# Two-layer hybrid encoder on one core: five small moves, and a copied first weight tile for each up run of the MLP

## The chip, the cores and the metric

The kernel runs on one core of one Trainium2 chip. A core has TensorE for matrix products (PE; its weight loads are shown as PEld), VectorE (DVE), ScalarE (ACT), GpSimd (POOL) and SyncE (SP), which run their own instruction streams and wait for each other on semaphores. Operands lie in SBUF, 128 partitions wide; sums of products lie in PSUM, in banks of 512 float32 per partition. The metric is the device time of one execution in microseconds, as the median of several runs.

## The reference

The computation is a two-layer encoder on 256 tokens of width 2048, with 256 memory tokens beside them. All is float32.

```python
def reference(x, mem, ...):
    m = rms_norm(mem, mem_norm)
    h = x
    for i in range(DEPTH):                      # 2 layers
        n = rms_norm(h, attn_norm[i])
        if i % 2 == 0:                          # layer 0: neighbourhood attention, 12 heads
            z = n @ a_w_in[j]                   # 2048 x 5120: q, k, v and the memory heads' q
            mix = neighbourhood_attention(q, k, v, a_rpb[j])
        else:                                   # layer 1: grouped-query attention, 12 heads, 4 kv heads
            z = n @ b_w_in[j]                   # 2048 x 3072
            mix = gqa_block_attention(rope(q), rope(k), v)
        km, vm = jnp.split(m @ w_mem_kv[i], 2, axis=-1)
        cross = memory_attention(qm, km, vm)    # 4 heads into the memory tokens
        h = h + jnp.concatenate([mix, cross], axis=-1) @ w_o[i]
        n = rms_norm(h, mlp_norm[i])
        h = h + jnp.square(jax.nn.relu(n @ w_up[i])) @ w_down[i]    # 2048 -> 8192 -> 2048
    return rms_norm(h, final_norm)
```

## The kernel before

**Products in three parts.** Every float32 operand is split into a high part (ACT, a Copy to the rounded type, line 377) and a low part (DVE, source minus high part, line 378): the function `split`. A product is then three matmuls: high by high, high by low, low by high. The function `products` (line 293) makes the S works, whose weights in PE are a 128x128 piece of the weight matrix and whose moving operand is 256 tokens wide: 16 steps k of three matmuls, 48 in a whole run. `m_products` (lines 272, 275, 276) makes the M works, where the activations are in PE and 512 columns of the weight matrix move.

**Stages.** The memory's K and V for both layers come first (to about 100 us), from `memT`, then layer 0's projections and attention, its output projection, its MLP (from about 438 us), then the same for layer 1, with its output projection at about 1300 us and its MLP at about 1364 us, and the final norm.

**The attention** of one head is three steps, `attend` (scores and softmax, lines 428 to 430), `attend2` (four transposes, line 454, then a split into `pT`) and `attend3` (the products `av` with the values, lines 462 to 464, and the split into `cat`). The steps are put between the works of the plan.

**The output projection** (`add_o`) is 16 M works: four blocks of 512 columns, two at a time, each with four chunks of the contraction. Each work has two halves (`hf` 0 and 1), a half holds two steps k. In the kernel before, the eighth work from the end, in layer 1, carries the mark `behind`: both of its splits are issued only after the last head's `pT` split. A finished block is added to `h` by DVE (line 725).

**The MLP** is cut into 8 parts of 1024 hidden columns. An up run is one S work of 128 hidden columns: `uh` and `ul` are the high and low parts of its weights, `hT` the normalised activations, `ps_u` the sum. Part 0 has eight up runs one after another. From part 1 on each up run stands between two groups of down products `p` (lines 894, 896, 897; 512 wide): 7 parts of 8 runs in each layer, 112 runs in all. The down products use a Strassen scheme, whose operands are `b` and its splits `bh`, `bl`, and the sums `t` and their splits `th`, `tl`; one of the sums is made by an accumulating DMA on POOL's queue (`b<-b`, line 866). In part 0 the splits of some up runs take rooms that later hold these, among them `u_th` and `u_tl`.

**What sets the order.** A list of grains (halves of works) is run in order, and each grain's load, pre-work and splits are issued some grains ahead (`SOON`, `SOONER`). SP's queue issues the weight loads in that order, and a load waits until its buffer is free. `past(fn)` issues the work of `fn` after given instructions. A tile is a buffer under a tag with a number of `bufs`; a new tile under the tag waits until the oldest buffer is free.

**Places.** Several constants in bytes set where an operand lies within its buffer. `hT` is an object of class `Shifted`: step k reads 256 float32 at a fixed step, except that the last k's high part lies `LAST_AT` = 224 bytes further. `ENTRY_AT` = 32 is how far the first 512 bytes of the low part lie from the usual place when an S work follows an M work (class `Entered`); there the low part's matmul also comes first. `STILL_AT`, `MOVING_AT` and `U_AT` place other halves.

**Start.** SP's queue issues the `gains`, then pieces of the memory `memT` and of the first three K weights `raw`, and the first products need both. `mem_stats` sums the squares of the memory over the partitions by matmuls with `ones`, into `pt_m` (line 582).

Of the kernel before, what the change touches and what calls it, by code (L numbers as in the profile page):

```python
# [10 lines left out]
F32 = mybir.dt.float32  # L11
F32R = mybir.dt.float32r
# [30 lines left out]

LAST_AT = 224

U_AT = 96

STILL_AT = 64

ENTRY_AT = 32  # L50
MASKED = -1e30


# [19 lines left out]
class Shifted:  # L73
# [5 lines left out]
    def __getitem__(self, key):  # L79
        _, k, s = key  # L80
        at = k * 512 + (s.start or 0)
        if k == KT - 1:

            at = k * 512 + (0 if s.start else SEQ + LAST_AT // 4)
        return self.room[:, at : at + SEQ]


class Entered:
# [19 lines left out]
def encoder_kernel(ctx: ExitStack, tc: tile.TileContext, t: dict, out: bass.AP):  # L108
# [38 lines left out]


    gains = const.tile([P, 5 * KT], F32, name="gains")
    nc.sync.dma_start(gains, t["gains"])  # L150
    h = keep.tile([P, NT, D], F32, name="h")
    mem0 = h.rearrange("p a b -> p (a b)")
    raws = [at.ring.tile([P, CH], F32, tag="raw", bufs=3, name=f"raw{c}") for c in range(FIRST_CHUNKS)]
# [34 lines left out]
    def halves_of(w):  # L188

        tiles = {}  # L190

        def load():
            tiles["raw"] = loaded(w.src, "U")

        def prep_early(hf):
            tiles[hf] = half_of_side(tiles["raw"], hf, MOVING_AT)

        def prep(hf):
            if hf == 0:
                n = plan.index(w)  # L200
                if n in soon:
                    tiles["raw"] = soon.pop(n)
                else:
                    tiles["raw"] = at.ring.tile([P, CH], F32, tag="raw", bufs=3, name="raw")
                    nc.sync.dma_start(tiles["raw"], w.src)
            src = tiles["raw"][:, hf * HALF : (hf + 1) * HALF]
            if w.behind:

                tiles[hf] = new_half(w.kind)
                past(lambda: split(*tiles[hf], src), box["pT"])  # L210
            elif w.kind == "S" and hf == 0 and plan[plan.index(w) - 1].kind == "M":
                tiles[hf] = entered_half(src)
            else:
                tiles[hf] = new_half(w.kind)
                split(*tiles[hf], src)

        def run(hf):
            if hf == 0:
                w.start(w)
            hi, lo = tiles.pop(hf)  # L220
            if w.kind == "S":
                s_products(w, hf * (KT // 2), KT // 2, hi, lo)
            else:
                for i in range(NT):
                    m_products(w, w.first + 2 * hf, 2, i, hi, lo, w.begins and hf == 0, w.last and hf == 1)

        def after():
            if w.last:
                w.done(w)
            if w.early == "last":  # L230
                to_work()

        if w.early:
            return [Grain(lambda: run(0), None, load, None, lambda: prep_early(0), SOON),
                    Grain(lambda: run(1), after, None, None, lambda: prep_early(1), SOON)]
        return [Grain(lambda: run(0), None, None, None, lambda: prep(0)),
                Grain(lambda: run(1), after, None, None, lambda: prep(1))]

    def new_half(kind):
        s = slice(STILL_AT // 4, STILL_AT // 4 + HALF) if kind == "S" else slice(0, HALF)  # L240
# [38 lines left out]

        products(w.ps, w.acts(), k0, nk, hi, lo)  # L280

    def products(ps, acts, k0, nk, hi, lo, keep_order=False):

        for j in range(nk):
            k = k0 + j
            s = slice(j * P, (j + 1) * P)
            parts = [(hi, slice(0, SEQ)), (hi, slice(SEQ, 512)), (lo, slice(0, SEQ))]
            if k == KT - 1:
                parts[:2] = parts[1::-1]
            elif j == 0 and isinstance(lo, Entered):  # L290
                parts = parts[2:] + parts[:2]
            for n, (x, part) in enumerate(parts):
                ins = nc.tensor.matmul(ps, x[:, s], acts[:, k, part], start=k == n == 0,  # L293
                                       stop=k == KT - 1 and n == 2)
                if keep_order and n == 0:
                    pin(ins)
# [126 lines left out]
    def attend(qT, kT, bias=None):  # L423
        sc_ps = at.att.tile([P, NT, SEQ], F32, tag="att", name="sc_ps")
        for s in range(NT):
            i = NT - 1 - s
            qh, ql = qT[:, i * P : (i + 1) * P], qT[:, SEQ + i * P : SEQ + (i + 1) * P]
            nc.tensor.matmul(sc_ps[:, s, :], qh, kT[:, :SEQ], start=True, stop=False)  # L428
            nc.tensor.matmul(sc_ps[:, s, :], qh, kT[:, SEQ:], start=False, stop=False)  # L429
            nc.tensor.matmul(sc_ps[:, s, :], ql, kT[:, :SEQ], start=False, stop=True)  # L430
        sc = at.work.tile([P, NT, SEQ], F32, tag="sc", bufs=3, name="sc")
        nm = small.tile([P, NT], F32, tag="nm", name="nm")
        sm = small.tile([P, NT], F32, tag="sm", name="sm")
        if bias is not None:
            over = bass.AP(tensor=bias.tensor, offset=bias.offset,
                           ap=[bias.ap[0], [2 * GRID_W, NT], [1, SEQ]])
            nc.vector.tensor_tensor(sc, sc_ps, over, op=ALU.add)
        src = sc_ps if bias is None else sc
        nc.vector.tensor_reduce(nm, src, axis=AX.X, op=ALU.max, negate=True)
        for s in range(NT):  # L440
            nc.scalar.activation(sc[:, s, :], src[:, s, :], AF.Exp, bias=nm[:, s : s + 1],
                                 accum_out=sm[:, s : s + 1])
        rs = small.tile([P, NT], F32, tag="rs", name="rs")
        nc.vector.reciprocal(rs, sm)
        for s in range(NT):
            nc.vector.tensor_scalar(sc[:, s, :], sc[:, s, :], rs[:, s : s + 1], None, op0=ALU.mult)
        return sc

    def attend2(sc):
        pt = at.att.tile([P, NT, SEQ], F32, tag="att", name="pt_a")  # L450
        for s in range(NT):
            i = NT - 1 - s
            for k in range(NT):
                nc.tensor.transpose(pt[:, k, i * P : (i + 1) * P], sc[:, s, k * P : (k + 1) * P], ident)  # L454
        pT = at.work.tile([P, 2, NT, SEQ], F32R, tag="pT", name="pT")
        box["pT"] = split(pT[:, 0], pT[:, 1], pt)
        return pT

    def attend3(pT, v, head, cat):
        av = at.att.tile([P, 512], F32, tag="att", name="av")  # L460
        for k in range(NT):
            nc.tensor.matmul(av[:, :SEQ], v(0, k), pT[:, 0, k, :], start=k == 0, stop=False)
            nc.tensor.matmul(av[:, :SEQ], v(0, k), pT[:, 1, k, :], start=False, stop=False)  # L463
            nc.tensor.matmul(av[:, :SEQ], v(1, k), pT[:, 0, k, :], start=False, stop=k == NT - 1)  # L464
        split(cat[:, head, :SEQ], cat[:, head, SEQ:], av[:, :SEQ])

    def attention(jobs, at, gap=1, lag=1, rest=0):
# [109 lines left out]

    def mem_stats():
        pt = at.att.tile([P, 512], F32, tag="att", name="pt_m")
        for i in range(NT):  # L580
            for b in range(2):
                nc.tensor.matmul(pt[:, i : i + 1], mem_sq[:, b * SEQ + i * P : b * SEQ + (i + 1) * P], ones[:, :1],
                                 start=b == 0, stop=b == 1)
        box["mem_col"] = keep.tile([P, NT], F32, name="mem_col")
        nc.vector.tensor_copy(box["mem_col"], rstd_of(pt[:, :NT], D, "mem"))
        box["mem_row"] = at.work.tile([P, SEQ], F32, tag="mem_row", bufs=1, name="mem_row")
        along_free(box["mem_col"], box["mem_row"])
# [163 lines left out]
    def add_o(layer):  # L751
        first, second, third, late = 3, 0, 1, 2
        for n in (0, 2):
            if n:
                order = [(b, c) for b in range(2) for c in range(4)]
            else:
                order = [(b, c) for b in range(2) for c in (first, second)]
                order += [(b, c) for c in (third, late) for b in range(2)]
            add_ms([([t[f"w_o{layer}"][nb * 4 + c] for c in range(4)], o_done(layer, nb)) for nb in (n, n + 1)],
                   parts_of("cat"), order)  # L760
            if n and layer:
                plan[-8].behind = True

# [19 lines left out]
    def up_grains(layer, part, m):  # L785
# [5 lines left out]
        def prep(hf):  # L791
# [9 lines left out]
                box["splits"].append(split(*own[hf], own["raw"][:, hf * HALF : (hf + 1) * HALF]))  # L801
            else:
                own[hf] = half_of_side(own["raw"], hf)

        def run(hf):
            if part == m == hf == 0:
                closed("cat", "ring")
                at.mlp = opened("mlp")
                box["z"] = [at.mlp.tile([P, 4, 512], F32, tag=f"z{q}", name=f"z{q}") for q in range(2)]
                box["z_set"] = set()  # L810
            if hf == 0:
                if part == 0:
                    own["ps"] = at.acc.tile([P, 512], F32, tag="acc", name="ps_u")[:, :SEQ]
                else:
                    own["ps"] = sum_of("up")[:, :SEQ]
            products(own["ps"], box["hT"], hf * (KT // 2), KT // 2, *own.pop(hf), keep_order=part > 0)

        def after():
            squared(layer, part, m, own["ps"])
# [519 lines left out]
```

## Time and profile before

| | |
|---|---|
| runs | 2041.18, 2039.49, 2039.66 us; median 2039.66 |
| profiled execution | 2039.6 us, its span 2037.8 us, mean granted clock 0.998 |
| PE busy | 2023.7 us, 99% of the span, 13116 matmuls |
| DVE busy | 1661.4 us, 82%, 2030 instructions |
| ACT busy | 1245.4 us, 61%, 1616 instructions |
| POOL busy | 119.3 us, 6% |
| DMA | 433.83 MB, mean 213 GB/s |

The span runs from the first to the last instruction on the core. A matmul's busy time in the table overlaps the next matmul's, since they are pipelined; what PE really pays for one is the interval from its start to the next one's start. In the chain of work that ended last, each piece has its start, its length and, after x, the number of instructions in it, so that length by count is that interval. In a timeline, what stands in brackets is the idle time before an instruction and what ended it. "Q" after an engine's name means its queue's issuing of a DMA.

### The profile page before, as it was taken

Reading aid. Unit: us, or ns where it says so; the run is one execution under the profiler, and the core shown is the slowest. Engines: PE = TensorE matmul, PEld = TensorE weight load, DVE = VectorE, ACT = ScalarE, POOL = GpSimd, SP = SyncE. Lnnn points to the kernel's source line nnn. Section 1 sums busy time; section 2 is a strip of 40 time slices with the busy share of each in tenths; the row PEclk is TensorE's granted clock in tenths of the full one; section 3 lists DMA queues with packets and bytes.
Section 4 is the critical chain, followed back from the end, with each engine's and each line's share of the span. In section 5 each row is a group of like instructions: output and inputs, shape, how many; then the busy total and the mean of one; then the engine's idle time right before and its main releaser. Section 6 shows DMA issues by size and latency. Waiting matters only on the chain.

```text
span 2037.8 us, 32567 instructions
## 1 busy us (share of the span) xinstructions
PE 2023.7 (99%) x13116; PEld 1838.0 (90%) x13116; DVE 1661.4 (82%) x2030; ACT 1245.4 (61%) x1616; POOL 119.3 (6%) x144
## 2 busy tenths in 40 slices
PE   9999999999999999999999999999999999999998
PEld 8999999899999999999988888889999999999996
DVE  6766666658998999989996667657999989999896
ACT  6655454556666666666655557556666666666664
POOL 0000000000000000000000001000000000000000
PEclk9999999999999999999999999999999999999999
DMA  7855555637777777777765544437777777777763
GB/s 282 305 186 183 178 176 180 243 136 229 233 232 230 222 238 231 224 235 228 232 204 212 178 168 146 178 140 234 233 233 231 219 243 220 232 238 228 235 215 127
DMA packets 77304, 433.83 MB, mean 213 GB/s; under 512 B 8673, under 2 KB 10337, under 8 KB 29665
## 3 DMA queue, kind: packets, MB, share of 16 engines
q1 hardware_dynamic: 59760, 399.25, 56.2%
q0 software_dynamic: 16816, 31.46, 8.9%
q8 instruction: 102, 1.67, 0.3%
q10 hardware_dynamic: 576, 1.05, 0.1%
q14 instruction: 50, 0.40, 0.1%
HBM read 398.17 MB, written 4.19 MB: 197 GB/s over the span
## 4 chain that ended last, share of the span: by engine, by line
PE 98%; DMA 1%; DVE 0%; issue 0%; ACT 0%; SPq 0%; POOLq 0%; POOL 0%; ACTq 0%; DVEq 0%
PE ps_u L293 34%; PE ps_s L293 10%; PE p L896 9%; PE p L894 9%; PE p L897 9%; PE ps_m L272 8%; PE ps_m L276 8%; PE ps_m L275 8%; PE pt_a L454 1%; PE pt_n L395 1%; PE av L463 0%; PE sc_ps L429 0%; PE sc_ps L428 0%; PE sc_ps L430 0%; PE av L464 0%
## 5 line engine op out<-in xcount | busy, mean ns | idle before, releaser
L293 PE MATMUL ps_u<-hT,uh 128*128 128x256 f32 x3904 | 676.6, 277 | 0.0
L293 PEld LDWEIGHTS ps_u<-hT,uh 128*128 128x128 f32 x3904 | 597.6, 188 | 9.1
L293 PE MATMUL ps_u<-hT,ul 128*128 128x256 f32 x1952 | 540.2, 277 | 0.0
L377 ACT ACTIVATE uh<-raw_U 128x1024 fp32r<-128x1024 f32 x266 | 282.2, 1062 | 281.1 <-PE ps_u L293 254.2
L378 DVE TENSOR_TENSOR lo<-raw,hi 128x1024 fp32r<-128x1024 f32 (+1 forms) x215 | 255.6, 1194 | 145.5 <-ACT hi L377 144.4
L293 PEld LDWEIGHTS ps_u<-hT,ul 128*128 128x128 f32 x1952 | 367.3, 188 | 0.0
L378 DVE TENSOR_TENSOR ul<-raw_U,uh 128x1024 fp32r<-128x1024 f32 x266 | 323.8, 1220 | 41.7 <-ACT uh L377 41.5
L377 ACT ACTIVATE hi<-raw 128x1024 fp32r<-128x1024 f32 (+1 forms) x215 | 222.3, 1039 | 196.6 <-PE ps_m L276 107.2
L377 ACT ACTIVATE bh<-b 128x2048 fp32r<-128x2048 f32 x112 | 215.3, 1922 | 115.0 <-PE p L897 90.4
L378 DVE TENSOR_TENSOR bl<-b,bh 128x2048 fp32r<-128x2048 f32 x112 | 256.2, 2288 | 16.9 <-ACT bh L377 16.8
L378 DVE TENSOR_TENSOR tl<-t,th 128x1536 fp32r<-128x1536 f32 x112 | 196.6, 1755 | 41.6 <-ACT th L377 40.6
L377 ACT ACTIVATE th<-t 128x1536 fp32r<-128x1536 f32 x112 | 166.7, 1488 | 38.7 <-PE p L897 37.5
L896 PE MATMUL p<-bl,a_s 128*128 128x512 f32 x448 | 174.6, 390 | 0.2
L897 PE MATMUL p<-bh,a_s 128*128 128x512 f32 x448 | 174.5, 390 | 0.0
L894 PE MATMUL p<-bh,a_s 128*128 128x512 f32 x448 | 174.3, 389 | 0.0
L866 POOL DMA_DIRECT2D b<-b x112 | 97.0, 866 | 1140.6 <-DVE t L865 1005.7
L293 PE MATMUL ps_s<-nT,hi 128*128 128x256 f32 x896 | 158.1, 279 | 0.0
L293 PEld LDWEIGHTS ps_s<-nT,hi 128*128 128x128 f32 x896 | 136.3, 188 | 0.2
L894 PE MATMUL p<-th,a_s 128*128 128x512 f32 x336 | 131.4, 391 | 0.0
L896 PE MATMUL p<-tl,a_s 128*128 128x512 f32 x336 | 131.2, 390 | 0.0
L897 PE MATMUL p<-th,a_s 128*128 128x512 f32 x336 | 130.7, 389 | 0.0
L293 PE MATMUL ps_s<-nT,lo 128*128 128x256 f32 x448 | 124.9, 279 | 0.0
(240 smaller groups left out, 3480.4 us busy)
## 6 DMA issues: line engine op xcount, KB each, us to landing
raw_U<-in_w_up SPq DMA_DIRECT2D x128, 1024.0 KB, 5.1
b<-in_w_pair SPq DMA_DIRECT2D x112, 1024.0 KB, 5.0
raw<-in_w_o SPq DMA_DIRECT2D x32, 1024.0 KB, 5.0
b<-b POOLq DMA_DIRECT2D x112, 256.0 KB, 3.4
raw<-in_w_b SPq DMA_DIRECT2D x21, 1024.0 KB, 5.1
raw<-in_w_av SPq DMA_DIRECT2D x12, 1024.0 KB, 5.0
raw<-in_w_aq SPq DMA_DIRECT2D x12, 1024.0 KB, 5.0
raw<-in_w_ak SPq DMA_DIRECT2D x12, 1024.0 KB, 5.0
```

The lines of the kernel that those rows point to most:

```text
L272: first = nc.tensor.matmul(w.ps[i], ah, hi[:, s], start=st, stop=False)
L275: nc.tensor.matmul(w.ps[i], ah, lo[:, s], start=False, stop=False)
L276: nc.tensor.matmul(w.ps[i], al, hi[:, s], start=False, stop=sp)
L293: ins = nc.tensor.matmul(ps, x[:, s], acts[:, k, part], start=k == n == 0, stop=k == KT - 1 and n == 2)
L377: first = nc.scalar.activation(dst_hi, src, AF.Copy)
L378: return first, nc.vector.tensor_tensor(dst_lo, src, dst_hi.bitcast(F32), op=ALU.subtract)
L395: nc.tensor.transpose(pt[:, b, i * P : (i + 1) * P], src(i, k), ident)
L454: nc.tensor.transpose(pt[:, k, i * P : (i + 1) * P], sc[:, s, k * P : (k + 1) * P], ident)
L866: nc.gpsimd.dma_start(b[:, 3, :], b[:, 1, :], accum_op=ALU.add)
L894: ins = nc.tensor.matmul(ps, a[:, 0, ai, :], hi[:, s], start=begins, stop=False)
L896: nc.tensor.matmul(ps, a[:, 0, ai, :], lo[:, s], start=False, stop=False)
L897: nc.tensor.matmul(ps, a[:, 1, ai, :], hi[:, s], start=False, stop=ends)
```

## The change

1. `gains` is loaded through ACT's queue instead of SP's.
2. `ENTRY_AT` goes from 32 to 160 bytes.
3. In part 0 of the up runs the last k's high part is read from a copy, `hT_l`, made by ACT once a layer; it lies 32 bytes into a buffer of the tag `a`. The class `Plain` stands for `hT` there (`hT0`). Parts 1 to 7 read `hT` as before.
4. In layer 1's output projection the last two works of the first half carry the mark `behind` instead of the eighth from the end. Only their second half's split is issued later, after the last head's softmax (`box["sm"]`) instead of its `pT` split, and of the last work's first half the second step k is issued after the last `av` product (`last_but_one`).
5. `mem_stats` adds the two halves of the squares on DVE and makes one matmul where there were two. These are plain float32, and the profile shows each as two rows, so that eight rows become four.
6. In parts 1 to 7, ACT copies the first 128 columns of each up run's weights (`raw`) once more, rounded to the high part, into `u_0`. The run's first matmul takes its weights from there. `COPY_AT` gives the copy's place, modulo 512 bytes, for each part and layer: fourteen different places. The tile has the tag `junk`, which has one buffer.

Apart from the two matmuls that are left out, PE's order of matmuls changes only near the end of layer 1's attention and, by one place, at a matmul of the memory's statistics. ACT has 115 instructions more (112 copies `u_0`, two copies `hT_l`, the issue of the DMA), DVE one more, SP one less.

```diff
-ENTRY_AT = 32
+LAST_COPY_AT = 32
+ENTRY_AT = 160
+COPY_AT = (None, 184, 288, 384, 440, 352, 416, 160), (None, 320, 192, 472, 176, 256, 200, 464)
+JUNK_AT = 480
...
+class Plain:
+    def __init__(self, shifted, last):
+        self.shifted, self.last = shifted, last
+    def __getitem__(self, key):
+        _, k, s = key
+        return self.shifted[key] if s.start or k < KT - 1 else self.last
...
-    nc.sync.dma_start(gains, t["gains"])
+    nc.scalar.dma_start(gains, t["gains"])
...
-            if w.behind:
+            if w.behind and hf == 1:
                 tiles[hf] = new_half(w.kind)
-                past(lambda: split(*tiles[hf], src), box["pT"])
+                past(lambda: split(*tiles[hf], src), box["sm"])
...
+                if w.behind and w.last and hf == 0:
+                    last_but_one(w, hi, lo)
+                    return
...
+    def last_but_one(w, hi, lo):
+        for i in range(NT):
+            m_products(w, w.first, 1, i, hi, lo, False, False)
+        with tc.issue_after(box["av"].ins):
+            for i in range(NT):
+                m_products(w, w.first + 1, 1, i, hi[:, 512:], lo[:, 512:], False, False)
...
-    def products(ps, acts, k0, nk, hi, lo, keep_order=False):
+    def products(ps, acts, k0, nk, hi, lo, keep_order=False, first=None):
...
-                ins = nc.tensor.matmul(ps, x[:, s], acts[:, k, part], start=k == n == 0,
+                x = first if n == j == 0 and first is not None else x[:, s]
+                ins = nc.tensor.matmul(ps, x, acts[:, k, part], start=k == n == 0,
...
+        nc.vector.tensor_tensor(mem_sq[:, :SEQ], mem_sq[:, :SEQ], mem_sq[:, SEQ:], op=ALU.add)
         for i in range(NT):
-            for b in range(2):
-                nc.tensor.matmul(pt[:, i : i + 1], mem_sq[:, b * SEQ + i * P : b * SEQ + (i + 1) * P], ones[:, :1],
-                                 start=b == 0, stop=b == 1)
+            nc.tensor.matmul(pt[:, i : i + 1], mem_sq[:, i * P : (i + 1) * P], ones[:, :1], start=True, stop=True)
...
-            if n and layer:
-                plan[-8].behind = True
+            if layer and n == 0:
+                plan[-1].behind = plan[-2].behind = True
...
+            if part and hf == 0:
+                s = slice((COPY_AT[layer][part] - JUNK_AT) % 512 // 4, None)
+                own["first"] = at.side.tile([P, 256], F32R, tag="junk", bufs=1, name="u_0")[:, s][:, :P]
+                nc.scalar.activation(own["first"], own["raw"][:, :P], AF.Copy)
...
+                last = at.mlp.tile([P, 14 * P], F32R, tag="a", bufs=6, name="hT_l")[:, LAST_COPY_AT // 4 :][:, :SEQ]
+                nc.scalar.activation(last, box["hT"][:, KT - 1, :SEQ].bitcast(F32), AF.Copy)
+                box["hT0"] = Plain(box["hT"], last)
...
-            products(own["ps"], box["hT"], hf * (KT // 2), KT // 2, *own.pop(hf), keep_order=part > 0)
+            products(own["ps"], box["hT" if part else "hT0"], hf * (KT // 2), KT // 2, *own.pop(hf), keep_order=part > 0,
+                     first=own.pop("first", None))
```

More of the change, by code (lines that the diff above doesn't have):

```diff
@@ L440, in attend @@
         for s in range(NT):
-            nc.scalar.activation(sc[:, s, :], src[:, s, :], AF.Exp, bias=nm[:, s : s + 1],
-                                 accum_out=sm[:, s : s + 1])
+            exp = nc.scalar.activation(sc[:, s, :], src[:, s, :], AF.Exp, bias=nm[:, s : s + 1],
+                                       accum_out=sm[:, s : s + 1])
         rs = small.tile([P, NT], F32, tag="rs", name="rs")
@@ L445, in attend @@
         for s in range(NT):
-            nc.vector.tensor_scalar(sc[:, s, :], sc[:, s, :], rs[:, s : s + 1], None, op0=ALU.mult)
+            times = nc.vector.tensor_scalar(sc[:, s, :], sc[:, s, :], rs[:, s : s + 1], None, op0=ALU.mult)
+        box["sm"] = exp, times
         return sc
@@ L455, in attend2 @@
         pT = at.work.tile([P, 2, NT, SEQ], F32R, tag="pT", name="pT")
-        box["pT"] = split(pT[:, 0], pT[:, 1], pt)
+        split(pT[:, 0], pT[:, 1], pt)
         return pT
@@ L463, in attend3 @@
             nc.tensor.matmul(av[:, :SEQ], v(0, k), pT[:, 1, k, :], start=False, stop=False)
-            nc.tensor.matmul(av[:, :SEQ], v(1, k), pT[:, 0, k, :], start=False, stop=k == NT - 1)
+            box["av"] = nc.tensor.matmul(av[:, :SEQ], v(1, k), pT[:, 0, k, :], start=False, stop=k == NT - 1)
         split(cat[:, head, :SEQ], cat[:, head, SEQ:], av[:, :SEQ])
```

## The prediction

> **What bounds the kernel now.** I read the page first: the busy shares, the granted clock by slices, and the chain that ended last.
>
> ```profile
> span 2037.8 us, 32567 instructions
> ...
> PE 2023.7 (99%) x13116; PEld 1838.0 (90%) x13116; DVE 1661.4 (82%) x2030; ACT 1245.4 (61%) x1616; POOL 119.3 (6%) x144
> ...
> PEclk9999999999999999999999999999999999999999
> ...
> PE 98%; DMA 1%; DVE 0%; issue 0%; ACT 0%; SPq 0%; POOLq 0%; POOL 0%; ACTq 0%; DVEq 0%
> ```
>
> TensorE (PE) carries 98% of the chain at an even granted clock. An edit here pays only if it takes matmuls away, takes PE's waits away, or shortens the interval from one matmul's start to the next. So the second view was the chain's longest pieces, each a time, a length and a count, which give that interval for the same 128x256 shape:
>
> ```profile
> 53.55 21.78 PE ps_s L293 x192
> ...
> 222.14 15.08 PE ps_s L293 x128
> ...
> 296.13 15.08 PE ps_s L293 x128
> ...
> 441.75 42.10 PE ps_u L293 x359
> 486.59 5.48 PE ps_u L293 x48
> 496.85 5.48 PE ps_u L293 x48
> ...
> 1030.41 5.48 PE ps_u L293 x48
> 1368.69 42.10 PE ps_u L293 x359
> ```
>
> 21.78 / 192 is 113.4 ns, but 15.08 / 128 is 117.8 ns and 42.10 / 359 is 117.3 ns. One shape, one clock, two speeds: call them quiet and stretched, 4.5 ns apart. The stretched pieces are the S runs at 222 and 296 us, which follow a value (M) work, and part 0 of each layer's up runs. The up runs of parts 1 to 7, 48 matmuls in 5.48 us, are quiet but for 5.48 - 48 x 0.1133 = 0.04 us. Where in the run that lies, the third view shows, PE's timeline at one run's start (time, length, and x2 where two were merged):
>
> ```profile
> 496.68 0.40 PE L293 MATMUL ps_u<-hT,uh 128*128 128x256 f32 x2
> 496.92 0.28 PE L293 MATMUL ps_u<-hT,ul 128*128 128x256 f32 x1
> ...
> 497.28 0.28 PE L293 MATMUL ps_u<-hT,ul 128*128 128x256 f32 x1
> ...
> 497.62 0.28 PE L293 MATMUL ps_u<-hT,ul 128*128 128x256 f32 x1
> ...
> 497.96 0.28 PE L293 MATMUL ps_u<-hT,ul 128*128 128x256 f32 x1
> ```
>
> From 496.68 to 497.28 five matmuls start in 0.60 us, 120 ns each; after that three take 0.34 us, 113.3 ns each. The run's first five matmuls lose 0.60 - 5 x 0.1133 = 0.033 us, and the rest of the 0.04 lies at its end. All 112 such runs can lose this.
>
> **The change part by part.** The sum is made against the profiled execution, 2039.6 us (span 2037.8 and 1.8 around it), which the median of the runs, 2039.66, matches.
>
> *Gains on ACT's queue, and the memory statistics.*
>
> ```profile
> 0.73 0.38 SPq L150
> ...
> 1.17 0.42 SPq L156
> ...
> 1.64 0.43 SPq L160
> ...
> 44.00 0.79 PE pt_m L582 x8
> ```
> ```profile
> 38.11 0.68 DVE L576 TENSOR_TENSOR mem_sq<-mem_sq,mem_y 128x512 f32<-128x512 f32 x1
> ```
>
> These are the chain's first steps: SP issues `gains`, then `memT`, then `raw`, and the first K product waits for that `raw`. With `gains` gone from SP the next issue starts at 0.73 in place of 1.17: -0.44 us, as long as `gains` itself, now issued by ACT, still lands before the first `memT` split, which is where it is first read. If that fails it is 0. I take -0.4. Eight `pt_m` rows of 0.79 us become four (two rows to each matmul): -0.4 us. The DVE add in their place has half the width of the 0.68 us one, so some 0.35 us (an estimate); DVE has five microseconds from 38.8, the end of the last such add, to 44.0. Without that cover it would cost its 0.35 and the gain would be nil.
>
> *The last k in part 0 (`hT0`).* The last k's high part is read from a copy at the place of all the others, so the moving operand no longer jumps by 224 bytes at the end of every part-0 run. At the quiet interval 359 matmuls take 40.68 us in place of 42.10: 1.4 us a layer, 2.8 in all. Run ends as in parts 1 to 7 (0.04 x 16 = 0.6) may stay: 2.2. Against it stands what is late next.
>
> ```profile
> 472.62 1.92 ACT L377 ACTIVATE bh<-b 128x2048 fp32r<-128x2048 f32 x1 [1.94 <-DMA b<-b]
> ...
> 475.39 0.36 ACT L831 ACTIVATE c<-ps_u 128x256 f32<-128x256 f32 x1
> ```
> ```profile
> 476.77 1.22 DVE L378 TENSOR_TENSOR u_tl<-raw_U,u_th 128x1024 fp32r<-128x1024 f32 x1
> ```
> ```profile
> 478.27 0.28 PE L293 MATMUL ps_u<-hT,u_tl 128*128 128x256 f32 x1
> ```
>
> Part 0's second-last half needs `u_tl`, ready at 477.99, and PE takes it at 478.27: 0.28 us of slack. That DVE work hangs on `bl` and `bh`, and `bh` on the DMA `b<-b`, which is not PE's pace. Up to there PE gains about 1.2 us in layer 0, but the DMA's issue moves forward with PE as well, so I give back 0.3 us (bounds 0 and 0.9, the whole of 1.2 less the slack). Net -1.9, from -2.8 to 0. The copy is one ACT instruction of 128x256 a layer, 0.36 us by the row at 475.39, needed fifteen k after the run's start.
>
> *ENTRY_AT.* The low part's first 512 bytes after a value work move by 128 bytes; no instruction is added. At stake are the two stretched pieces: 2 x (15.08 - 128 x 0.1133) = 1.15 us and some pieces behind them. Two of layer 0's five such entries are stretched at one common place, so the place alone does not decide. Bounds -1.6 and +0.6 (a quiet entry that turns stretched); I take -1.0.
>
> *Behind.* Near the end of layer 1's attention, filler work moves:
>
> ```profile
> 1309.67 0.38 PE L463 MATMUL av<-pT,vb 128*128 128x256 f32 x1 [0.34 <-DVE pT L378]
> ...
> 1311.11 0.50 PE L272 MATMUL ps_m<-hi,cat 128*128 128x512 f32 x1 [0.58 <-ACT cat L377]
> ```
> ```profile
> 1310.56 4.84 DMA raw_U<-in_w_up
> 1315.43 1.07 ACT uh L377
> 1316.52 0.40 DVE ul L378
> 1316.92 0.56 issue
> 1317.66 0.69 DVE h L725
> 1318.40 0.50 PE ps_m L272
> ```
>
> The first pair of stalls, 0.9 us, can be filled by matmuls that are ready. But the chain to 1318.40 starts from a transfer, and that transfer from the last `av` product, whose pool it takes over: `uh`, then `ul` stand on ACT and DVE ahead of the `h` add that frees the bank for the next M block. Filler put ahead of the last `av` empties the place behind it, where 1.55 us are idle now. So the next block still starts some 8 us behind that `av`, which moves by less than 0.7 us either way, the sum of the shifts that I can see (half a 0.9 us stall gained, as much filler lost). I take 0, bounds -0.7 and +0.7.
>
> *The copy of a run's first high weights.* ACT gets 112 more instructions, half of a 128x256's width, so at most 0.36 us each, 40 us in all. Each stands ahead of its `uh` split:
>
> ```profile
> L377 ACT ACTIVATE uh<-raw_U 128x1024 fp32r<-128x1024 f32 x266 | 282.2, 1062 | 281.1 <-PE ps_u L293 254.2
> ...
> L378 DVE TENSOR_TENSOR ul<-raw_U,uh 128x1024 fp32r<-128x1024 f32 x266 | 323.8, 1220 | 41.7 <-ACT uh L377 41.5
> ```
> ```profile
> 487.00:1030.00 543.00, 542.90 (x3653) 498.57 (x3652) 504.00 (x539) 354.25 (x353) 46.15 (x53) 1.00 0.74 230
> ```
>
> ACT idles 281.1 / 266 = 1.06 us ahead of each `uh`, on PE, for a buffer, not for data; and it is 65% busy in parts 1 to 7 (354 of 543 us, the fourth busy figure). That hides the copies. DVE, at 504 of 543, does follow: up to 0.3 us later `ul` a run, which its 39 us idle just hold. So the cost lies on PE alone: a first matmul with its weights at another place. If a place suits, the 33 ns go: 112 x 0.033 = -3.7 us. If it starts the stretched interval, the run costs 48 x 4.5 - 40 = 176 ns more, 1.41 us for the 8 runs of a part. Bounds -3.7 and +19.7 (14 parts). The trace shows this junction at one pair of places only, quiet; nearest are the other junctions, where part 0 and two of five entries are stretched. I take two of 14 places stretching (+2.8), and half of the other twelve saving the 33 ns (6 x 8 x 0.033 = -1.6): +1.2.
>
> Sum: -0.4 - 0.4 - 1.9 - 1.0 + 0 + 1.2 = -2.5 us, thus 2037.0.
>
> The Trainium skill ("SBUF — State Buffer", section "Who interferes with whom") says that moving operand and weight load have a read port each, and that PE never waits on anyone. By that rule the places of operands cost nothing, and the sum would be -0.8; the 113.4 and 117.8 ns above, with one shape and one clock, speak against it.
>
> **The rivals.** *No place stretches:* -3.7 for the five other edits, and -1.6 to -3.7 for the copies, so 2032.2 to 2034.3. For it: all 112 runs are quiet now. Against it: the four stretched pieces elsewhere, and fourteen different places.
>
> *Many places stretch* (the other side). With n stretching places and half of the rest saving, the total is -3.7 + 1.41 n - 0.13 (14 - n): six give +3.7, seven +5.3, fourteen +16. From seven the kernel is measurably slower, 2044.9. For it: the stretched pieces follow an odd place at a run's start or end and stay so to their last matmul. Against it: they come from two kinds of junction only.
>
> *Places do nothing:* the two speeds have another cause, the stretched ones stay, and gains and statistics alone are left: -0.8, 2038.8. That is the change not doing what it says. For it: five entries at one place were not alike.
>
> *DVE becomes late:* if its 39 us do not lie where `ul` needs them, 0.3 us show at a part of the 112 runs; beyond one in four (+8.4 - 3.7) it is slower, about 2044. Against it: the waits of `ul` on ACT are 41.5 us now and PE does not stop.
>
> **How the numbers follow.** A difference under 0.2%, 4.1 us, is about what a measurement of this kernel cannot tell from none. Mixed places, one to four stretching, 0.40: its own range 2034.6 to 2041.2 (one stretching -4.0, four +0.6, and a microsecond on either side for the other edits); 0.12 of it ends beyond 4.1 us faster. No place stretching 0.27, all faster. Many stretching 0.17: 0.04 same (five or six), 0.13 slower. Places do nothing 0.10, same. DVE late 0.06, slower. So faster 0.39, same 0.42, slower 0.19. The range 2032.0 to 2045.0 leaves out about 0.07 below, where the bounds of several edits meet, and 0.12 above, eight stretching places or more.
>
> **What would show it.** Gains: the first SP issue in the chain is `memT`, and the first `ps_s` comes 0.4 us earlier. Statistics: `pt_m` x4. `hT0`: part 0 at 113 to 114 ns a matmul, with a wait for `u_tl` near 478. ENTRY: the pieces of 128 matmuls at 14.5 us. Behind: no stall at the last `av`, a longer one ahead of the next M block. Copies: the pieces of 48 in parts 1 to 7, at 5.44 us where a place suits, 5.48 where nothing changes, 5.65 where it is stretched, alike within a part. The prediction is wrong if those pieces are alike in all parts, if PE waits for `ul`, or if the next M block after the attention starts over a microsecond earlier.

## The result, and the profile after

The changed kernel takes 2052.84 us (2052.60 to 2054.98, four runs) against 2040.07 us (2039.49 to 2041.18, four runs): 12.8 us or 0.63% more by the medians; the ratio on record is 1.0065, with the 95% interval 1.0052 to 1.0077. That is outside the predicted range of 2032.0 to 2045.0, and on the other side of no change.

The page of the changed kernel has the same shape as before, PE first by far and at an even clock:

```profile
span 2051.1 us, 32732 instructions
...
PE 2036.8 (99%) x13112; PEld 1848.5 (90%) x13112; DVE 1664.1 (81%) x2031; ACT 1269.2 (62%) x1730; POOL 119.3 (6%) x144
...
PEclk9999999999999999999999999999999999999999
...
PE 96%; DMA 1%; DVE 1%; ACT 1%; issue 1%; SPq 0%; POOLq 0%; POOL 0%; DVEq 0%; ACTq 0%
```

So the loss is in the matmuls' intervals again, and the chain's longest pieces show where. Columns are start, length, what, and the count; of the pieces of 48 the first of each group of like ones stands here.

```profile
9.54 20.52 PE ps_s L321 x178
52.77 22.61 PE ps_s L321 x192
...
222.21 15.09 PE ps_s L321 x128
...
296.22 15.09 PE ps_s L321 x128
...
441.84 18.84 PE ps_u L321 x166
467.03 5.17 DMA b<-b
...
485.95 5.65 PE ps_u L321 x48
...
653.20 5.46 PE ps_u L321 x48
...
735.02 5.65 PE ps_u L321 x48
...
818.70 5.45 PE ps_u L321 x48
...
900.51 5.66 PE ps_u L321 x48
...
1375.35 18.84 PE ps_u L321 x166
...
1419.57 5.65 PE ps_u L321 x48
...
1670.14 5.46 PE ps_u L321 x48
...
1752.06 5.67 PE ps_u L321 x48
...
1835.74 5.46 PE ps_u L321 x48
...
1917.66 5.65 PE ps_u L321 x48
```

All eight runs of a part are alike. A part's eight runs take 8 x 10.23 = 81.8 us with their down products (653.20 to 735.02) where the pieces are 5.46, and 8 x 10.46 = 83.7 us (485.95 to 569.63) where they are 5.65. Before, the period was (1009.51 - 486.59) / 51 = 10.25 us, over runs without a stall between them. Four parts are quiet, 3 and 5 in layer 0 (places 384 and 352), 4 and 6 in layer 1 (176 and 200); the other ten are stretched, each at some 1.5 us.

The one further row of the kernel before that a balance by stages needs is the start of layer 1's part 1, from the chain between 1408 and 1440 us:

```profile
1413.54 5.48 PE ps_u L293 x48
```

| stretch | before, us | after, us | difference |
|---|---|---|---|
| start to the second set of K products | 53.55 | 52.77 | -0.78 |
| from there to part 0 of layer 0 | 388.20 | 389.07 | +0.87 |
| part 0, layer 0 | 44.84 | 44.11 | -0.73 |
| parts 1 to 7 of layer 0, and layer 1 up to its part 0 | 882.10 | 889.40 | +7.30 |
| part 0, layer 1 | 44.85 | 44.22 | -0.63 |
| parts 1 to 7 of layer 1, to the end of the span | 624.26 | 631.53 | +7.27 |

The sum is 13.3 us, the difference of the spans. The two stages with the copies lose 14.6, all the rest gains 1.3. Of the 14.6, 0.1 has nothing to do with the copies: from the last up run of layer 0 to part 0 of layer 1 it is 1368.69 - 1050.92 = 317.77 us before and 1375.35 - 1057.48 = 317.87 after.

### The profile page after: what moved, and what is told of

Same layout as the page of the kernel before. It is cut to its first block, busy times and chain, and to the rows that moved or that the text cites. A ratio compares the mean times of both kernels' runs of the same rounds, so it can differ in the third digit from the quotient of the medians.

```text
span 2051.1 us, 32732 instructions
## 1 busy us (share of the span) xinstructions
PE 2036.8 (99%) x13112; PEld 1848.5 (90%) x13112; DVE 1664.1 (81%) x2031; ACT 1269.2 (62%) x1730; POOL 119.3 (6%) x144
## 4 chain that ended last, share of the span: by engine, by line
PE 96%; DMA 1%; DVE 1%; ACT 1%; issue 1%; SPq 0%; POOLq 0%; POOL 0%; DVEq 0%; ACTq 0%
PE ps_u L321 33%; PE ps_s L321 10%; PE p L934 9%; PE p L932 9%; PE p L935 9%; PE ps_m L299 8%; PE ps_m L302 8%; PE ps_m L303 8%; PE pt_a L483 1%; PE pt_n L423 1%; DMA b<-b 1%; PE av L492 0%; PE av L493 0%; PE sc_ps L457 0%; PE sc_ps L456 0%
## 5 line engine op out<-in xcount | busy, mean ns | idle before, releaser
L321 PEld LDWEIGHTS ps_u<-hT,uh 128*128 128x128 f32 x3780 | 580.9, 189 | 5.1
```

Of the source, the lines that this page charges most:

```text
L321: ins = nc.tensor.matmul(ps, x, acts[:, k, part], start=k == n == 0, stop=k == KT - 1 and n == 2)
```

## The experiments

### Are the copies the cause, and is it their place?

Theory 1: the place of the first matmul's weights sets the interval of the whole run, whatever the part. Rivals: the copies' work on ACT and DVE delays PE; or the same place acts differently by part and layer. Three kernels tell these apart. The first leaves the copies out:

```diff
-            if part and hf == 0:
+            if False:
```

> The five other edits alone; the 112 copies and their use are left out, every run's first matmul reads uh again. Theory 1 (the place of the first matmul's weights decides the interval of the whole run): the loss sits in parts 1 to 7 alone, where the trace of the changed kernel moved from -0.64 to +6.68 us in layer 0 and from +6.04 to +13.2 us in layer 1, 14.5 us together; without the copies all pieces of 48 are back at 5.48 us and the time is 2040.07 + 13.2 - 14.5 = about 2038.8. Rival (the copies' work on ACT and DVE delays PE): the same 2038.8, so this run tells only that the loss is the copies'. Rival (one of the five edits stretches parts 1 to 7): about 2052.

Measured: 2039.9 us, ratio 1.000 (0.9991 to 1.0008). The pieces of 48 are back at 5.48 us, so the loss is the copies'. The first of them, from the chain of this kernel:

```profile
485.98 5.48 PE ps_u L321 x48
```

The time is 1.1 us above what was expected, and its eleven values lie unusually wide, 2037.57 to 2043.83; what the profiled execution shows of this is told further down.

The second keeps all copies, at one place:

```diff
-COPY_AT = (None, 184, 288, 384, 440, 352, 416, 160), (None, 320, 192, 472, 176, 256, 200, 464)
+COPY_AT = (None, 352, 352, 352, 352, 352, 352, 352), (None, 352, 352, 352, 352, 352, 352, 352)
```

> All 14 parts take the place 352, which was quiet in one part (5.45 us a run). The copies stay, 112 of them, with ACT's work as it was. Theory 1 (place alone): every piece of 48 at 5.45 us, about 0.025 us a run under the kernel before, 2.8 us in all: 2038.8 - 2.8 = 2036.0. Rival (ACT's and DVE's work): no better than 2052. Rival (place and part together, by the phase at which a run is entered): only some parts quiet, between 2040 and 2052.

Measured: 2035.16 us, ratio 0.9979 (0.9970 to 0.9987). The chain of this kernel has pieces of 5.45 us throughout; the first and the last that it lists:

```profile
52.81 22.61 PE ps_s L321 x192
...
485.85 5.45 PE ps_u L321 x48
...
833.55 5.45 PE ps_u L321 x48
```

ACT's busy time is 1269.1 us, as in the changed kernel (1269.2), and 2052.84 - 2035.16 = 17.7 us are gone. The copies' work on ACT and DVE is therefore hidden, and the place is what costs. The third kernel moves each place to the other layer, and in reverse order, so that all but two (440 and 176, in part 4) change the part as well:

```diff
+COPY_AT = (None, 464, 200, 256, 176, 472, 192, 320), (None, 160, 416, 352, 440, 384, 288, 184)
```

> The fourteen places stay but change layers and are reversed in order: layer 0 has 464, 200, 256, 176, 472, 192, 320, layer 1 has 160, 416, 352, 440, 384, 288, 184. Theory 1 (place alone): the quiet parts are 2 and 4 in layer 0 (200, 176) and 3 and 5 in layer 1 (352, 384), the other ten at 5.65 us, the time again about 2053. Rival (place and part together): the quiet parts stay 3 and 5 in layer 0 and 4 and 6 in layer 1, or fall in no pattern.

Measured: 2052.26 us in one run. From the chain of this kernel, parts 1, 2, 3 and 4 of layer 0, and 3 and 5 of layer 1:

```profile
485.71 5.65 PE ps_u L321 x48
...
569.28 5.46 PE ps_u L321 x48
...
651.20 5.67 PE ps_u L321 x48
...
734.88 5.46 PE ps_u L321 x48
...
1586.26 5.45 PE ps_u L321 x48
...
1751.74 5.46 PE ps_u L321 x48
```

The same four places are quiet in their new parts, and 256 is again the longest at 5.67. The verdict goes with the place, not with part or layer.

### The map of places

Two more kernels put 28 other places in the fourteen parts. The second also sets `ENTRY_AT` to 96.

> Fourteen other places: layer 0 has 8, 16, 24, 40, 48, 56, 72 in parts 1 to 7, layer 1 has 80, 104, 112, 120, 136, 144, 152. If what counts is the place modulo 256, the quiet ones known so far are 96, 128, 176, 200 and 224, the stretched ones 0, 32, 64, 160, 184, 192, 208 and 216. Theory 1 with zones: 8 to 80 stretched, as 0, 32 and 64 are; 104, 112 and 120, between 96 and 128, quiet; 136 to 152 open: 8 to 11 stretched parts, 2048 to 2053. Rival (no zones, since 176, 184, 192 and 200 alternate): quiet and stretched mixed along 8 to 80 as well.

> Fourteen places: layer 0 has 88, 168, 232, 240, 248, 0, 128 in parts 1 to 7, layer 1 has 432, 456, 96, 368, 280, 408, 376; and ENTRY_AT is 96. Theory (the place modulo 256 alone decides): 0 and 280 stretched, as 256 and 24 were; 128, 432, 456, 96, 368, 408 and 376 quiet, as 384, 176, 200, 352, 112, 152 and 120 were. 88, 168, 232, 240 and 248 are new; 88 lies between 80 (stretched) and 96 (quiet), the others between stretched and quiet ones. With 2 to 7 stretched parts: 2038 to 2048. Rival (modulo 512): some of the nine differ from their twins. ENTRY_AT is read by the stage: 21.8 us for the 192 matmuls at 53 us and 14.5 us for the two pieces of 128 where 96 is a quiet place, 22.6 and 15.1 where not.

Measured: 2043.71 and 2040.44 us, one run each. The first is below the 2048 to 2053 us that zones would give: four of its parts are stretched, not eight or more. Places that are equal modulo 256 behave alike (eleven pairs, 128 and 384 or 24 and 280 among them), so the table goes by that. The piece of 48 in us, for every multiple of 8, with 224 from the kernel before:

| place modulo 256 | 5.45 to 5.48 us | 5.65 to 5.67 us |
|---|---|---|
| 0 to 56 | 8, 16, 48 | 0, 24, 32, 40, 56 |
| 64 to 120 | 72, 88, 96, 104, 112, 120 | 64, 80 |
| 128 to 184 | 128, 136, 144, 152, 168, 176 | 160, 184 |
| 192 to 248 | 200, 224, 248 | 192, 208, 216, 232, 240 |

Eighteen are quiet and fourteen stretched, and there is nothing between 5.48 and 5.65: a run is in the one way or in the other from its start to its end. Of the zones that I expected one is there, the quiet one, from 88 to 152. The table holds for the other weights and `hT` where the changed kernel has them. Of the changed kernel's fourteen places ten stand in the right column.

### The other edits, one by one

In the changed kernel the 192 K products at 53 us went from 21.78 to 22.61 us, and the pieces at 222 and 296 us stayed stretched. One kernel undoes `ENTRY_AT`:

```diff
-ENTRY_AT = 160
+ENTRY_AT = 32
```

> As the kernel with the place 352 in all parts (2035.16 us), but ENTRY_AT is 32 again. Theory (160 stretches the second layer's K products of the memory, 192 matmuls at 22.61 in place of 21.78 us, and mends nothing at 222 and 296 us): those 192 are back at 21.8 us, the pieces of 128 stay at 15.08, the time falls by 0.8 us to 2034.4. Rival (the shorter memory statistics right before, not ENTRY_AT, bring that stage in at another phase): 22.6 us stay, 2035.2.

Measured: 2034.94 us, ratio 0.9976 (0.9967 to 0.9986), too near to 2035.16 to tell by the times. The chain tells:

```profile
52.01 21.78 PE ps_s L321 x192
...
220.82 15.08 PE ps_s L321 x128
```

The 192 are back at 21.78, so 160 is what stretched them: 0.83 us lost, and the piece at 222 us (220.82 here) is stretched with 32 and with 160. With `ENTRY_AT` = 96, in the kernel that completes the map, all three are quiet:

```profile
52.93 21.77 PE ps_s L321 x192
...
221.53 14.52 PE ps_s L321 x128
...
294.54 14.52 PE ps_s L321 x128
```

The copies by themselves are tried in the kernel before, at 352, without the five other edits:

```diff
+COPY_AT = 352
...
+            if part and hf == 0:
+                s = slice((COPY_AT - JUNK_AT) % 512 // 4, None)
+                own["first"] = at.side.tile([P, 256], F32R, tag="junk", bufs=1, name="u_0")[:, s][:, :P]
+                nc.scalar.activation(own["first"], own["raw"][:, :P], AF.Copy)
```

> The kernel before with the 112 copies at the place 352 and none of the five other edits. Theory (the copy at a quiet place saves some 25 ns a run by itself): 112 x 0.025 = 2.8 us, 2037.2, pieces of 48 at 5.45 us. Rival (the gain of the kernel with one place came from the five edits, which are worth more than their own stages show): 2040.

Measured: 2037.03 us, ratio 0.9984 (0.9975 to 0.9994); 5.45 us a piece, and part 0 still stretched, as in the chain of this kernel:

```profile
441.74 42.17 PE ps_u L297 x359
486.66 5.45 PE ps_u L297 x48
```

Well placed, the idea is worth some 3 us: 2037.03 against 2040.22 for the kernel before in the same set of runs, and by the interval of the ratio between 1 and 5. Last, the wait at the end of part 0. In the changed kernel the first part-0 piece runs at 18.84 / 166 = 113.5 ns, but the chain then leaves PE, through the transfer at 467.03 and these:

```profile
472.22 1.93 ACT bh L405
...
476.39 1.23 DVE u_tl L406
...
477.66 1.42 PE ps_u L321 x10
```

The next kernel, with the place 352 and `ENTRY_AT` = 32, issues the splits `bh` and `bl` after `u_th` and `u_tl`:

```diff
-        def behind(fn):
+        def behind(fn, at=4):
-            return (lambda: past(fn, box["splits"][-4])) if part == 0 and n < 2 else fn
+            return (lambda: past(fn, box["splits"][-at])) if part == 0 and n < 2 else fn
...
-        return [Grain(lambda: run("first", FIRST), lambda: after(FIRST), load, behind(pre), behind(prep_first),
+        return [Grain(lambda: run("first", FIRST), lambda: after(FIRST), load, behind(pre), behind(prep_first, 2),
```

> As e5_entry_back, and at the end of part 0 the first splits bh and bl are issued after u_th and u_tl, not ahead of them. Theory (what hT0 gained was given back in part where PE waits for u_tl behind bl, 0.5 us in each layer): that wait goes and bl, with some 2 us to spare, becomes no new one: 1.0 us less, 2033.4. Rival (bl comes too late for the first down products): the wait moves to the first p and the time stays at 2034.4.

Measured: 2034.55 us, ratio 0.9974 (0.9963 to 0.9985). By the times this is not told from 2034.94; by the chain the wait is gone, and no other has come in its place: from the first piece of part 0 to part 1 it takes 43.50 us in both layers, here in layer 0:

```profile
440.97 40.71 PE ps_u L321 x359
484.47 5.45 PE ps_u L321 x48
```

40.71 us is 359 x 113.4 ns, 1.39 under the 42.10 of before.

### The best of both, and the filler near 1310 us

The best kernel joins the place 352, `ENTRY_AT` = 96 and the later `bh` and `bl`. Beside it runs the same kernel with the change at the end of layer 1's attention undone.

> As e8_u_tl_first, with ENTRY_AT 96, which was quiet at every entry of layer 0 in the run of the last fourteen places. The stage from 222 to 440 us should lose 2 x (15.08 - 14.52) + 2 x (6.36 - 6.12) = 1.6 us more. From the traces: e8 without its long transfer near 1310 us stands at about -3.6 us there and -5.9 us at the end, so -7.5: about 2032.5 us, against 2040.1.

> As e9_best, but the change to the filler work near 1310 us is undone: the eighth work from the end carries the mark again and waits for the pT split. Theory (the next M block starts about 8 us behind the last av product either way, so this edit is worth nothing): the same time as e9_best within 0.5 us, and the same place of the M block's start against the stage's start. Rival (the new filler matters when the transfer raw_U takes longer): e9_best and this one differ by a microsecond or more in some executions.

Measured: 2031.23 us, ratio 0.9958 (0.9945 to 0.9970), and 2030.98 us, ratio 0.9958 (0.9944 to 0.9972). The best kernel is 8.7 us under the kernel before, and the new filler is worth nothing that shows. The timelines show PE's wait ahead of the next M block, with the new filler and then with the old:

```profile
1313.59 0.50 PE L299 MATMUL ps_m<-hi,cat 128*128 128x512 f32 x1 [1.55 <-DVE h L753]
```
```profile
1312.45 0.50 PE L296 MATMUL ps_m<-hi,cat 128*128 128x512 f32 x1 [1.60 <-DVE h L750]
```

1.55 and 1.60 us, as 1.55 in the kernel before.

### What the place is measured against

Three kernels with the changed kernel's own fourteen places: `uh` and `ul` moved by 64 bytes, `hT` moved by 64 bytes, and both with the copies moved along.

> The changed kernel with its own fourteen places, and the buffers uh and ul of parts 1 to 7 moved by 64 bytes (32 in place of 480, modulo 512); the moving operand stays. Theory A (what counts is the copy's place against the run's own moving operand): the same four parts are quiet (3 and 5 in layer 0, 4 and 6 in layer 1), about 2053. Theory B (it counts against the place of the weights that follow): place p behaves as p - 64 did, so 120, 224, 64, 120, 32, 96, 96 and 0, 128, 152, 112, 192, 136, 144 modulo 256: stretched in parts 3 and 5 of layer 0 and 1 and 5 of layer 1 only, about 2042. Third way: the moved rest is itself stretched in all parts, 2057.

> The changed kernel with its own fourteen places, and hT moved by 64 bytes (224 in place of 160), with its copy hT_l; uh and ul stay. Theory A (the copy's place against the moving operand): place p behaves as p - 64 did: stretched in parts 3 and 5 of layer 0 and 1 and 5 of layer 1 only, about 2042. Theory B (against the weights that follow, or in itself): the same four quiet parts as in the changed kernel, about 2053. Third way: the moved hT stretches every run, part 0 too, 2057.

> The changed kernel with hT, uh and ul of parts 1 to 7, and the fourteen copies all moved by 64 bytes, so that they lie to each other as in the changed kernel; the down products' operands stay. Theory A (only the distances between a run's own operands count): the same four parts are quiet, 3 and 5 in layer 0 and 4 and 6 in layer 1, the others at 5.65 us, about 2053. Theory B (the address itself, or the distance to the down products' operands before the run, counts): another pattern, or all parts stretched as when hT or uh moved alone (2066 to 2080).

Measured: 2066.51, 2079.79 and 2053.12 us, one run each. In the first two every piece is stretched (5.69 to 5.76 and 5.74 to 5.75 us), so they cannot tell theory A from B, and both times lie beyond all that was expected. They show that the places of the following weights and of the moving operand count as well as that of the first weights. (The 2079.79 us also hold a late transfer and a halved clock, of which the last section tells.) In the third, where all distances within a run are the old ones, the pattern is another: eight parts are quiet, 3, 5, 6 and 7 in layer 0 and 3, 4, 5 and 6 in layer 1, and part 0 is stretched (43.26 us for 359). From its chain, parts 1 and 5 to 7 of layer 0:

```profile
488.14 5.65 PE ps_u L321 x48
...
821.16 5.47 PE ps_u L321 x48
...
903.55 5.46 PE ps_u L321 x48
...
985.79 5.46 PE ps_u L321 x48
```

So the distances within a run do not decide alone: the address itself, or the distance to something that stayed, as the down products' operands did, has a part. Which of them stays open. That the time is the 2053 us of theory A is luck. From the first piece of part 0 to part 1 it takes 46.0 and 45.8 us in place of 44.1 and 44.2, 3.5 more in all, and the stages with the copies, with their four further quiet parts, take 3.3 less.

The last kernel needs no copy: the whole of `uh` and `ul` lies at 96 modulo 256, in the best kernel with the copies left out.

```diff
-                own[hf] = half_of_side(own["raw"], hf)
+                own[hf] = half_of_side(own["raw"], hf, 128 if part else 0)
```

> The fastest kernel so far (2031.2 us) without copies, and the whole of uh and ul of parts 1 to 7 at the place 96 modulo 256, the copies' quiet place, by moving them 128 bytes. Theory A (the first weights' place sets the interval): quiet runs, 2031 us, and no copies. Rival (the weights that follow have a place of their own that must fit the moving operand, as moving them by 64 bytes stretched every run): pieces of 48 at 5.65 us or more, 2050 and up.

Measured: 2031.79 us, ratio 0.9957 (0.9941 to 0.9974), its pieces at 5.46 us:

```profile
482.53 5.46 PE ps_u L321 x48
```

It is not told from the best kernel by its time, and it has no copies `u_0`, 112 instructions fewer on ACT. A place that suits the whole buffer does what the copies do.

## Why the prediction was wrong, point by point

*The copies* were the failed step, "I take two of 14 places stretching (+2.8), and half of the other twelve saving the 33 ns": +1.2 us. Ten of 14 stretched, and the copies' stages lost 14.6 us. The mechanism was right, and the prices were near: a stretched run was put at 176 ns more than before, 5.65, and it costs 10.46 - 10.25 = 0.2 us a period; a quiet one was put at 33 ns less and saves 10.25 - 10.23, some 25 ns. What was mis-sized is the number of stretching places. The two of 14 rest on no row: the working sets the other junctions beside them, and of those two of five entries and part 0 were stretched, 40 to 50%, which would have been six or seven places. Even that is a share of junctions, not of places. The map gives 14 of 32, which is six of 14, and the changed kernel's ten are more than this share. The case named "Many places stretch" (ten: -3.7 + 14.1 - 0.5 = +9.9) had a chance of 0.17 where the map would have given it most. The bounds of -3.7 and +19.7 held.

The Trainium skill ("SBUF — State Buffer", section "Who interferes with whom") gives PE one read port for the moving operand and an independent one for the weight load, and has it wait on no other engine; that section does not speak of places. The working concluded from it that places would cost nothing, and gave that 0.10. The runs refute it: 5.45 against 5.65 us, with nothing but the place changed.

*ENTRY_AT*, -1.0 with bounds -1.6 and +0.6, came out at +0.83, from 22.61 against 21.78 us. The forecast took a gain at the two stretched pieces; they stayed, and an entry that was quiet turned, which the upper bound had too low by 0.2. The caution in it, that one place had not decided at five entries, was right: a place has to be tried at each junction.

*hT0* was put at -1.9 and gave -0.73 - 0.63 = -1.4. The mending itself was right (2.2 forecast; 113.5 ns a matmul from the first run on). The stall that it gives back was put at 0.3 in all. It took 0.6 us in layer 0 alone: up to the first piece of part 1 the changed kernel needs 44.11 us, the kernel with the later `bh` and `bl` 484.47 - 440.97 = 43.50. I let the DMA's issue move forward with PE and counted one layer; the wait for `u_tl` grew by most of what PE gained beyond its 0.28 us of slack, and layer 1, at 44.22 us, has it too. With 0.6 and 0.7 us the stalls exceed the bound of 0.9 as well.

*Gains and statistics*, -0.4 each: the first K products end at 9.54 + 20.52 = 30.06 in place of 8.49 + 21.88 = 30.37, so -0.3, and -0.78 with the statistics. Right within what one execution tells: in the kernels that start like the changed one the second set of K products begins between 52.01 and 53.20 us, and at 53.93 in one whose clock was halved at the start; in the two with the old start it begins at 53.55 and 53.54.

*Behind*, 0: right in size. From the last up run of layer 0 to the next M block it is 1325.07 - 1057.48 = 267.59 us, 1318.40 - 1050.92 = 267.48 before, and the transfer that the block hangs on still follows the last `av` product. One sign did not come: the wait ahead of the block is not longer, but 1.24 us in the changed kernel and 1.55 against 1.60 in the pair made for it. The waits of 0.34 and 0.58 us at the last `av` are gone, but PE now waits 0.72 us at 1312.11 for a split of the filler itself.

*DVE late*, the rival at 0.06: refuted by the kernel with one place, which has the same copies and 5.45 us throughout. The 39 us of idle time hold 53 x 0.3 = 16 us more than twice; "just" was a misreading.

So the sum of the five other edits, -3.7, was -1.3: 1.8 us of the gap lie at `ENTRY_AT` and 0.5 at `hT0`. The other 13.4 us, 14.6 against the 1.2 of the sum, are the copies' places. The times of the kernel with the five edits alone, 2039.9 against 2040.01 us, cannot tell -1.3 from nothing (the interval is -1.8 to +1.6 us). The sum itself, 2039.6 - 2.5, is 2037.1 and not 2037.0.

## What to carry to other kernels

Where one engine carries the chain, divide the length of the chain's long pieces by their counts: the same shape at 113.4 and 117.8 ns is a place to look for. Operand places were such a cause here, worth 4 to 6% of a run of 256-wide matmuls (5.45 against 5.65 and 5.76 us), and they could not be derived from a few junctions; a kernel with a different place in every part reads a dozen of them in one profile, and the best of them can then be used everywhere. Such a table is a measurement, not a version to keep.

## What the runs showed of the hardware that was not expected

*The first weight load can set a whole run.* With `hT` and the other weights where the changed kernel has them, the place of one 128x128 weight load, the first of 48, moved by as little as 8 bytes, sets the interval of all that follow: 5.45 to 5.48 or 5.65 to 5.67 us, nothing between, and alike for all eleven pairs of places 256 bytes apart. Not every slow start lasts: in the kernel before, five matmuls at 120 ns were followed by quiet ones. Why a place stretches stays open.

*After waits of some 2 us and more PE's clock was halved for 3.4 us.* The kernel with the five edits alone was profiled in an execution in which the transfer of `raw_U` near 1310 us took 7.09 us instead of 4.84. The windows of that execution (length, then busy time and count for PE, PEld, DVE, ACT and POOL, then the granted clock, the DMA's share and GB/s) and its timeline:

```profile
1314.00:1319.80 5.80, 2.53 (x13) 1.76 (x11) 1.90 (x3) 2.99 (x4) 0.00 (x0) 1.00 0.87 357
...
1321.00:1324.00 3.00, 3.00 (x8) 2.32 (x8) 3.00 (x5) 2.91 (x8) 0.00 (x0) 0.50 0.49 120
```
```profile
1319.78 0.50 PE L299 MATMUL ps_m<-hi,cat 128*128 128x512 f32 x1 [3.27 <-DVE h L753]
...
1321.50 0.63 PE L299 MATMUL ps_m<-hi,cat 128*128 128x512 f32 x1
1321.92 0.63 PE L302 MATMUL ps_m<-lo,cat 128*128 128x512 f32 x1
```

PE waited 3.27 us, and about 1.2 us after it went on the clock fell to 0.50 for 3.4 us, in which the interval of 512-wide matmuls was 0.43 us (1321.50 to 1321.92) in place of 0.23. The kernel with the later `bh` and `bl` had the same after a shorter wait, by its timeline and its windows:

```profile
1315.52 0.49 PE L299 MATMUL ps_m<-hi,cat 128*128 128x512 f32 x1 [2.04 <-DVE h L753]
```
```profile
1316.00:1318.00 2.00, 2.00 (x8) 1.52 (x7) 2.00 (x4) 2.00 (x4) 0.00 (x0) 0.58 0.07 29
```

So had the kernel with `hT` alone moved, after a transfer of 7.48 us, and, at its first K products, the first of the two kernels of the map, where the clock fell within 0.1 us of the wait's end:

```profile
1339.21 0.50 PE L299 MATMUL ps_m<-hi,cat 128*128 128x512 f32 x1 [3.70 <-DVE h L753]
```
```profile
7.33 1.50 PE L321 MATMUL ps_s<-memT,hi 128*128 128x256 f32 x4 [1.97 <-ACT hi L405]
```

In thirteen of the sixteen profiled executions, the kernel before among them, the wait ahead of the M block near 1320 us was 1.00 to 1.69 us, and the clock stayed up after it. The first execution lost 7.09 - 4.84 = 2.3 us to the transfer, and some 1.6 to the clock (eight matmuls at 0.43 in place of 0.23 us). That such executions make the wide spread of the times of the kernel with the five edits is likely, but not shown: it was profiled once, and why the transfer took longer wasn't tried. The Trainium skill ("TensorE: Matmul & The Clock Gate", section "HAM oscillation — how this bites in real kernels") warns of idle gaps above about 3.4 us; 1.97 and 2.04 us sufficed here.
